# Gram operands of an RWKV-7 front made unswapped in one 128-partition product, swapped later by 64-column matmuls

## The chip, the cores and the metric

The kernel runs on one core of a Trainium2 chip. TensorE (PE) multiplies matrices; its weight loads are listed apart as PEld. VectorE (DVE) and ScalarE (ACT) work on tiles in on-chip memory, GpSimd (POOL) and SyncE (SP) mostly issue transfers. The metric is the time of one execution on the device, in microseconds (us); lower is better.

## The reference, cut to what matters

One decoder layer: an RWKV-7 branch and an S5 branch are merged by gates, and a gated MLP follows. The part around the change is the RWKV-7 recurrence, with 8 heads of 64 channels and 1024 time steps:

```python
def step(S, inp):
    r_t, w_t, k_t, v_t, a_t, b_t = inp
    sa = jnp.einsum('bhij,bhj->bhi', S, a_t)
    S = (S * w_t[:, :, None, :] + sa[..., None] * b_t[:, :, None, :]
         + v_t[..., None] * k_t[:, :, None, :])
    return S, jnp.einsum('bhij,bhj->bhi', S, r_t)
```

It is called with a = -kk and b = kk * a_gate, where kk is the key, scaled and normalised in each head, and with a key k that the gate has scaled as well. All numbers are float32.

## The kernel before, in words

The recurrence is computed in chunks of 64 time steps. In each chunk the products of all pairs of steps are needed: of the "b" and "k" vectors of step s with the "a" and "r" vectors of step t. These are the Gram matrices, 128 by 128 for a head and a chunk, since (b, k) and (a, r) are each laid side by side, 64 columns each.

The work is cut into four groups `d` (two halves of the sequence by two groups of four heads). A group holds two pairs of heads, `u` = 0 and 1, and eight chunks, `c` = 0 to 7. In a tile the first head of a pair (head 0) lies in partitions 0 to 63 and the second (head 1) in partitions 64 to 127; `HS[0]` and `HS[1]` are these two slices, of partitions or of columns.

`rwkv_front` (L680 ff.) runs once for each `d` and `u`, eight times in all. On DVE it writes `ar` (a in columns 0 to 63 of a chunk, r in 64 to 127: L736 and L726) and `bk` (b and k: L739 and L728). For head 0, b stands in columns 0 to 63 of `bk` and k in 64 to 127; for head 1 they stand the other way round. A DVE instruction writes the same columns in all its partitions, so L728 and L739 are each made of two instructions, one for each head, of 64 partitions by 512 elements.

Then PE makes the Gram matrices in two halves of four chunks (`q` = 0, 1): L750 issues, for each chunk, one product for head 0 and one for head 1, each with 64 rows of weights and 128 columns, 128 elements moving. DVE masks them into `gr` (L752), POOL sends parts of `gr` away (L758) for the inversion (`rwkv_inv`, on DVE).

`rwkv_nat` (L767 ff.) runs once for each `d`: for each `u` and `q`, PE transposes four chunks of `bk` (L780), ACT copies the result to `bkn` (L781), and PE does the same with v (L787, L788, L790), which ACT copies to `UV` (L792). Then `rwkv_level` and `rwkv_chain` run the recurrence over the chunks.

All matmul operands here are float32, and one such matmul makes two records in the trace; a transpose makes one. The large matmuls of the projections (L179 to L181) are of another type and make one record each.

The order of PE's instructions is written by `drive`: it hands the turn to several generators by their estimates of time (the numbers that they yield) and fills PE's free time with pieces of the projections. The instructions of one piece stay together. The order on the other engines comes from a scheduler.

Of the kernel before, what the change touches and what calls it, by code (L numbers as in the profile page):

```python
# [13 lines left out]
ALU = mybir.AluOpType  # L14
# [13 lines left out]
HS = (slice(0, 64), slice(64, 128))  # L28
# [44 lines left out]
class Kern:  # L73
# [606 lines left out]
    def rwkv_front(self, d, u, i):  # L680

        nc, V, G, A = self.nc, self.nc.vector, self.nc.gpsimd, self.nc.scalar
        mm = nc.tensor.matmul
        o = slice(d["th"] * 512, d["th"] * 512 + 512)
        p = 2 * d["g"] + u
        gf = d["gr"][:, u].rearrange("p c h t -> p (c h t)")
        kk, yb, pe = gf[:, 0:512], gf[:, 512:1024], gf[:, 1024:1544].rearrange("p (c t) -> p c t", t=65)

        def c64(x):
            return x.rearrange("p (c t) -> p c t", t=64)  # L690

        def ld(src, q=nc.sync):
            t = self.tg("ld", NLD)
            q.dma_start(t, src[:, o])
            return t
        k, tz, ta, r = (ld(x) for x in (self.RKV[4 + p], self.TZ[p], self.TA[p], self.RKV[p]))

        self.squared = A.activation(kk, k, AF.Square, scale=self.vec("k_k", p))
        if d["g"] == d["th"] == 0:
            self.tc.add_manual_dep(self.squared.ins, self.last_wh.ins.name, ORDER)  # L700
        yield 0, T_LD
        yield 0, lambda: self.nat >= i - 1 and self.outs >= i - 1
        if "ar" not in d:
            self.rwkv_operands(d)
        ar, bk = d["ar"][:, u], d["bk"][:, u]
        ar0, ar1 = ar[:, :, 0:64], ar[:, :, 64:128]
        bk0, bk1 = [[bk[HS[h], :, HS[h ^ j]] for h in range(2)] for j in range(2)]
        st = self.rp((128, 4, 2))
        for tb in range(4):
            mm(st[:, tb], kk[:, tb * 128:(tb + 1) * 128], self.cst("ones_bd")[:, 0:128:64], start=tb == 0, stop=True,  # L710
               skip_group_check=True)
        sv = self.small.tile([128, 8], F32, tag="sv", name=self.nm("sv"), bufs=2)
        V.tensor_scalar(sv, st.rearrange("p a b -> p (a b)"), 1e-24, None, ALU.max)
        y = self.rsqrt(sv, 8, "pr")

        scan = V.tensor_tensor_scan(tz, self.cst("smask"), tz, 0.0, ALU.mult, ALU.add)
        if self.levelled is not None:
            self.tc.add_manual_dep(scan.ins, self.levelled.ins.name, ORDER)
        G.memset(pe[:, :, 0:1], 1.0)
        A.activation(pe[:, :, 1:65], c64(tz), AF.Exp, scale=-0.5 * CDEC)  # L720
        A.activation(tz, tz, AF.Exp, scale=0.5 * CDEC)
        G.tensor_copy(d["pt"][:, :, u], pe[:, :, 64])
        tk = yb
        A.activation(tk, ta, AF.Identity, bias=self.ka_1[:, p:p + 1], scale=self.ka_h[:, p:p + 1])
        V.tensor_tensor(tk, tk, k, ALU.mult)
        V.tensor_tensor(ar1, c64(r), pe[:, :, 1:65], ALU.mult)  # L726
        for h, sl in enumerate(HS):
            V.tensor_tensor(bk1[h], c64(tk)[sl], c64(tz)[sl], ALU.mult)  # L728
        V.scalar_tensor_tensor(r, r, self.vec("r_k", p), tk, ALU.mult, ALU.mult)
        yield 0.9, T_KN, 1.5  # L730
        kb = self.rp()
        A.copy(c64(yb), y.unsqueeze(2).to_broadcast([128, 8, 64]))
        for tb in range(4):
            nc.tensor.transpose(kb[:, tb * 128:(tb + 1) * 128], yb[:, tb * 128:(tb + 1) * 128], self.cst("ident"))
        V.scalar_tensor_tensor(kk, k, self.vec("k_k", p), kb, ALU.mult, ALU.mult)
        V.scalar_tensor_tensor(ar0, c64(kk), -1.0, pe[:, :, 0:64], ALU.mult, ALU.mult)  # L736
        V.scalar_tensor_tensor(kk, ta, 1.0, kk, ALU.add, ALU.mult)
        for h, sl in enumerate(HS):
            V.scalar_tensor_tensor(bk0[h], c64(kk)[sl], 0.5, c64(tz)[sl], ALU.mult, ALU.mult)  # L739
        v = ld(self.RKV[8 + p], G)  # L740
        yield 0.5, T_BK

        gm = self.cst("gmask").unsqueeze(1).to_broadcast([128, 4, 128])
        for q in range(2):
            yield 0, lambda: self.now >= self.masked
            self.masked = self.now + 1.8 + T_GR
            ps = [self.rp((128, 4, 128)) for h in range(2)]
            for c in range(4 * q, 4 * q + 4):
                for h, sl in ((0, slice(0, 64)), (1, slice(64, 128))):
                    mm(ps[h][:, c % 4], bk[sl, c], ar[sl, c], start=c % 4 == 0, stop=True, skip_group_check=True)  # L750
            for h in range(2):
                V.tensor_tensor(d["gr"][:, u, 4 * q:4 * q + 4, h], ps[h], gm, ALU.mult)  # L752
            yield 1.8, T_GR
        for blk in range(2):
            md = d["md"][u, blk].rearrange("(c h) q t -> h q c t", h=2)
            for h in range(2):
                sl = slice(64 * h + 32 * blk, 64 * h + 32 * blk + 32)
                nc.gpsimd.dma_start(md[h], d["gr"][sl, u, :, h, 32 * blk:32 * blk + 32])  # L758

        pb = self.rp()  # L760
        mm(pb, self.cst("ones_bd"), r, start=True, stop=True)
        V.tensor_tensor(r, pb, v, ALU.mult)
        nc.gpsimd.dma_start(d["bv"][u], r)
        d["v"][u] = v
        yield 0.55, 1.5

    def rwkv_nat(self, d):  # L767

        nc, A = self.nc, self.nc.scalar
        mm = nc.tensor.matmul  # L770
        ident = self.cst("ident")
        o = slice(d["th"] * 512, d["th"] * 512 + 512)
        d["bkn"] = self.tg("bkn", 1, (128, 2, 8, 128))
        d["UV"] = self.tg("UV", 1, (128, 8, 2, 2, 64))
        for u in range(2):
            v = d["v"][u]
            for q in range(2):
                ps = self.rp((128, 4, 128))
                for c in range(4):
                    nc.tensor.transpose(ps[:, c], d["bk"][:, u, 4 * q + c], ident)  # L780
                A.copy(d["bkn"][:, u, 4 * q:4 * q + 4], ps)  # L781
                yield 0.5, 0
                ps = self.rp((128, 4, 128))
                for c in range(4):
                    b = 4 * q + c
                    if b == 0:
                        mm(ps[64:128, c], v[:, 0:64], ident, start=True, stop=True, skip_group_check=True)  # L787
                        mm(ps[0:64, c], v[:, 448:512], ident, start=True, stop=True, skip_group_check=True)  # L788
                    else:
                        nc.tensor.transpose(ps[:, c], v[:, 64 * b - 64:64 * b + 64], ident)  # L790
                for h in range(2):
                    A.copy(d["UV"][HS[1 - h], 4 * q:4 * q + 4, h, u], ps[HS[1 - h], :, HS[h]])  # L792
                yield 0.5, 0.8
# [1367 lines left out]
```

## Time and profile before

| what | value |
|---|---|
| time, median of 3 runs | 1545.53 us (1538.57 to 1547.73) |
| the profiled execution: its time, its span | 1553.39 us, 1551.6 us |
| busy: PE, DVE, ACT | 96%, 74%, 47% |
| fronts: first and last Gram record (L750) | 302.7 us, 609.2 us |
| `rwkv_nat`: first and last transpose of `bk` (L780) | 324.6 us, 681.0 us |
| mean granted clock of TensorE | 0.980 |

Times within the profile count from the span's start. A row of a group of instructions gives line, engine, operation, the tiles written and read, the shapes and the count; then, behind the bar, the busy time in us and the mean duration of one in ns; then the idle time before them and what ended it. For a matmul the shape of the weights comes first, rows by columns (64\*128), then the operand that moves. The durations of matmuls overlap, because they are pipelined, so what one costs is read from the distance of the starts in the timeline: there a row gives the start, the time to the end of the last record in it, and the count of records.

### The profile page before, as it was taken

What the parts mean: (1) busy time and instruction counts of PE and PEld (TensorE: products, weight loads), DVE (VectorE), ACT (ScalarE), POOL (GpSimd) and SP (SyncE); (2) the same over time, 40 slices, a digit from 0 to 9 for tenths busy, and PEclk for the clock granted to TensorE, in tenths of its full rate; (3) what the DMA queues carried; (4) which work ended last, traced back from release to release, by engine and by line L of the source; (5) the groups of instructions that cost most, each with busy time, mean ns of one, the idle gap of its engine ahead of it and who ended that gap; (6) DMA issues with size and microseconds to landing.
All of it is one profiled execution on the core that took longest, in us unless ns stands there. A gap on an engine that the chain in (4) does not pass through costs nothing.

```text
span 1551.6 us, 23464 instructions
## 1 busy us (share of the span) xinstructions
PE 1486.4 (96%) x8622; PEld 1186.8 (76%) x8622; DVE 1150.6 (74%) x2112; ACT 725.3 (47%) x1200; POOL 180.1 (12%) x340
## 2 busy tenths in 40 slices
PE   7997999999999998989999999999999999999997
PEld 5786888777677676666778788888888888788775
DVE  7878874756456486784668869788888887698667
ACT  6454543331353344546534456455555555443452
POOL 0022111123130214030110011000000000000000
PEclk9998999999999999999999999999999999999999
DMA  6354344343433446452355576233333336953722
GB/s 211 113 151 131 100 134 151 130 139 101 147 108 110 123 129 172 144 168 69 115 184 166 182 265 204 95 109 115 123 102 110 121 115 204 330 172 122 239 74 109
DMA packets 121124, 224.44 MB, mean 145 GB/s; under 512 B 30976, under 2 KB 37120, under 8 KB 121008
## 3 DMA queue, kind: packets, MB, share of 16 engines
q1 hardware_dynamic: 90144, 153.98, 31.9%
q0 software_dynamic: 21024, 64.71, 12.6%
q10 hardware_dynamic: 9840, 4.24, 1.0%
q8 instruction: 68, 1.11, 0.3%
q14 instruction: 48, 0.39, 0.1%
HBM read 163.37 MB, written 57.41 MB: 142 GB/s over the span
## 4 chain that ended last, share of the span: by engine, by line
PE 71%; DVE 12%; DMA 7%; issue 5%; ACT 4%; SPq 0%; POOL 0%; DVEq 0%; ACTq 0%; POOLq 0%
PE gm L179 9%; PE gm L180 8%; PE gm L181 7%; PE rp L1578 5%; PE rp L1580 5%; PE rp L1579 5%; DMA st<-in_w_down_dram 2%; PE mm L1578 2%; PE mm L1580 2%; PE mm L1579 2%; PE ch L180 2%; PE ch L179 2%; PE ch L181 2%; PE mm L179 2%; PE mm L180 2%
## 5 line engine op out<-in xcount | busy, mean ns | idle before, releaser
L179 PE MATMUL gm<-hh,wh 128*128 128x512 f32 x688 | 292.6, 425 | 2.7 <-DVE last L1046 2.0
L180 PE MATMUL gm<-hl,wh 128*128 128x512 f32 x688 | 273.6, 398 | 1.7 <-DVE hl L245 1.6
L181 PE MATMUL gm<-hh,wl 128*128 128x512 f32 x688 | 273.1, 397 | 0.0
L159 ACT CAST wh<-wf 128x512 fp32r<-128x512 f32 x178 | 109.8, 620 | 176.4 <-PE gm L180 99.7
L160 DVE TENSOR_TENSOR wl<-wf,wh 128x512 fp32r<-128x512 f32 x178 | 122.5, 692 | 87.6 <-ACT wh L159 86.2
L179 PEld LDWEIGHTS gm<-hh,wh 128*128 128x128 f32 x688 | 131.7, 191 | 36.1 <-ACT spt L893 2.4
L181 PEld LDWEIGHTS gm<-hh,wl 128*128 128x128 f32 x688 | 131.5, 191 | 29.2
L180 PEld LDWEIGHTS gm<-hl,wh 128*128 128x128 f32 x688 | 132.1, 192 | 25.9 <-DVE hl L245 3.5
L1756 PE MATMUL d<-xl,wh 128*128 128x512 f32 x308 | 120.4, 391 | 5.4 <-DVE xl L245 5.4
L1755 PE MATMUL d<-xh,wh 128*128 128x512 f32 x308 | 120.1, 390 | 0.0
L1757 PE MATMUL d<-xh,wl 128*128 128x512 f32 x308 | 119.9, 389 | 0.0
L1578 PE MATMUL rp<-t,h 128*128 128x512 f32 x252 | 98.3, 390 | 1.6 <-ACT p L1592 1.6
L1580 PE MATMUL rp<-t,l 128*128 128x512 f32 x252 | 98.1, 389 | 0.0
L1579 PE MATMUL rp<-t,h 128*128 128x512 f32 x252 | 98.0, 389 | 0.0
L1756 PEld LDWEIGHTS d<-xl,wh 128*128 128x128 f32 x308 | 57.8, 188 | 19.2 <-DVE xl L245 7.4
L245 DVE TENSOR_TENSOR l<-r,h 128x1024 fp32r<-128x1024 f32 (+1 forms) x40 | 38.9, 971 | 39.5 <-ACT h L244 39.4
L1755 PEld LDWEIGHTS d<-xh,wh 128*128 128x128 f32 x308 | 57.8, 188 | 12.3 <-DVE p L1707 0.2
L244 ACT CAST h<-r 128x1024 fp32r<-128x1024 f32 (+1 forms) x40 | 33.9, 849 | 70.7 <-PE rp L1579 67.0
L1757 PEld LDWEIGHTS d<-xh,wl 128*128 128x128 f32 x308 | 57.8, 188 | 11.9
L1599 DVE SCALAR_TENSOR_TENSOR y<-zv,vecs,y 128x1023 f32<-128x1023 f32 (+1 forms) x42 | 53.8, 1280 | 10.2 <-ACT y L1597 10.2
L1578 PEld LDWEIGHTS rp<-t,h 128*128 128x128 f32 x252 | 47.3, 188 | 12.2 <-ACT p L1592 2.5
L1580 PEld LDWEIGHTS rp<-t,l 128*128 128x128 f32 x252 | 47.3, 188 | 9.9
(473 smaller groups left out, 3338.0 us busy)
## 6 DMA issues: line engine op xcount, KB each, us to landing
r<-in_w_up_dram SPq DMA_DIRECT2D x42, 512.0 KB, 3.5
wf<-in_w_in_dram SPq DMA_DIRECT2D x72, 256.0 KB, 3.0
st<-in_w_down_dram SPq DMA_DIRECT2D x55, 256.0 KB, 4.5
st<-ACT SPq DMA_DIRECT2D x44, 256.0 KB, 4.2
ACT<-y POOLq DMA_DIRECT2D x21, 512.0 KB, 2.9
GT<-ev POOLq DMA_DIRECT2D x32, 256.0 KB, 3.4
wf<-in_w_br_dram SPq DMA_DIRECT2D x32, 256.0 KB, 2.7
wf<-in_w_out_dram SPq DMA_DIRECT2D x32, 256.0 KB, 2.8
```

The lines of the kernel that those rows point to most:

```text
L159: self.last_wh = nc.scalar.copy(h[:, :n], f[:, :n])
L160: low = nc.vector.tensor_tensor(l[:, :n], f[:, :n], h[:, :n].bitcast(F32), ALU.subtract)
L179: mm(ps, a, xh[k], start=a0, stop=False)
L180: mm(ps, a, xl[k], start=False, stop=False)
L181: mm(ps, b, xh[k], start=False, stop=z0)
L1578: mm(ps, wh[:, c], xh, start=first and k == 0, stop=False, skip_group_check=True)
L1579: mm(ps, wh[:, c], xl, start=False, stop=False, skip_group_check=True)
L1580: mm(ps, wl[:, c], xh, start=False, stop=k == 3, skip_group_check=True)
L1599: V.scalar_tensor_tensor(y[:, lag:], z[:, 0:1024 - lag], self.vec(nme, i), y[:, lag:], ALU.mult, ALU.add)
L1755: mm(ps, wh[:, c], xh[:, x], start=start, stop=False, skip_group_check=True)
L1756: mm(ps, wh[:, c], xl[:, x], start=False, stop=False, skip_group_check=True)
L1757: mm(ps, wl[:, c], xh[:, x], start=False, stop=stop, skip_group_check=True)
```

## The change

DVE writes `bk` unswapped, b in columns 0 to 63 and k in 64 to 127 for both heads, so that L728 and L739 become one instruction each, of 128 partitions by 512 elements. The swap of head 1 moves to PE.

In the Gram products head 0 keeps its one matmul of 64 by 128. Head 1 gets two of 64 by 64: the k columns give partitions 0 to 63 of the result, the b columns partitions 64 to 127.

In `rwkv_nat` each transpose of a chunk becomes three matmuls with a part of the identity matrix as the operand that moves: one for head 0 (64 rows by 128 columns of weights) and two for head 1 (64 by 64), which swap its halves.

```diff
-        bk0, bk1 = [[bk[HS[h], :, HS[h ^ j]] for h in range(2)] for j in range(2)]
+        bk0, bk1 = bk[:, :, 0:64], bk[:, :, 64:128]
...
-        for h, sl in enumerate(HS):
-            V.tensor_tensor(bk1[h], c64(tk)[sl], c64(tz)[sl], ALU.mult)
+        V.tensor_tensor(bk1, c64(tk), c64(tz), ALU.mult)
...
-        for h, sl in enumerate(HS):
-            V.scalar_tensor_tensor(bk0[h], c64(kk)[sl], 0.5, c64(tz)[sl], ALU.mult, ALU.mult)
+        V.scalar_tensor_tensor(bk0, c64(kk), 0.5, c64(tz), ALU.mult, ALU.mult)
...
-                for h, sl in ((0, slice(0, 64)), (1, slice(64, 128))):
-                    mm(ps[h][:, c % 4], bk[sl, c], ar[sl, c], start=c % 4 == 0, stop=True, skip_group_check=True)
+                kw = dict(start=c % 4 == 0, stop=True, skip_group_check=True)
+                mm(ps[0][:, c % 4], bk[HS[0], c], ar[HS[0], c], **kw)
+                for j in range(2):
+                    mm(ps[1][HS[j], c % 4], bk[HS[1], c, HS[1 - j]], ar[HS[1], c], **kw)
...
-                    nc.tensor.transpose(ps[:, c], d["bk"][:, u, 4 * q + c], ident)
+                    x = d["bk"][:, u, 4 * q + c]
+                    mm(ps[:, c, 0:64], x[HS[0]], ident[HS[0], HS[0]], start=c == 0, stop=True, skip_group_check=True)
+                    for j in range(2):
+                        mm(ps[HS[j], c, 64:128], x[HS[1], HS[1 - j]], ident[HS[1], HS[1]], start=False, stop=True, skip_group_check=True)
```

Three places in the order of instructions show it. In these rows the shape is that of the result, partitions by elements; "x2" stands for two alike in a row; `rp` is a bank of results, `gm` one of a projection.

PE at the first half of the first Gram of the program, before: the last projection matmuls ahead of it, and the first chunk (the last two rows come three more times).

```order
L181 MATMUL gm_2939<-hh_395,wl_2842 128x512
L179 MATMUL gm_2939<-hh_400,wh_2841 128x512
L180 MATMUL gm_2939<-hl_401,wh_2841 128x512
L181 MATMUL gm_2939<-hh_400,wl_2842 128x512
L750 MATMUL rp_2952<-ar_2733,bk_2734 128x128
L750 MATMUL rp_2953<-ar_2733,bk_2734 128x128
```

The same place now (again the last two rows come three more times; L748 is head 0, L750 head 1).

```order
L181 MATMUL gm_2935<-hh_395,wl_2840 128x512
L179 MATMUL gm_2935<-hh_400,wh_2839 128x512
L180 MATMUL gm_2935<-hl_401,wh_2839 128x512
L181 MATMUL gm_2935<-hh_400,wl_2840 128x512
L748 MATMUL rp_2948<-ar_2733,bk_2734 128x128
L750 MATMUL rp_2949<-ar_2733,bk_2734 64x128 x2
```

The place in the order is the same; head 1's one product of 64 by 128 has become two of 64 by 64, and products of the two sizes now alternate.

PE at the first piece of `rwkv_nat`, before: the transposes of four chunks of `bk`, then those of v.

```order
L181 MATMUL gm_3080<-hh_415,wl_3075 128x512
L780 MATMUL rp_3225<-csts,bk_2734 128x128 x4
L787 MATMUL rp_3231<-csts,ld_2883 64x128
L788 MATMUL rp_3231<-csts,ld_2883 64x128
L790 MATMUL rp_3231<-csts,ld_2883 128x128 x3
L179 MATMUL gm_3080<-hh_420,wh_3074 128x512
```

The same place now, from the fourth chunk on (the first two rows stand there three times before, behind the L181 of the projection).

```order
L781 MATMUL rp_3237<-csts,bk_2734 128x64
L783 MATMUL rp_3237<-csts,bk_2734 64x64 x2
L790 MATMUL rp_3251<-csts,ld_2880 64x128
L791 MATMUL rp_3251<-csts,ld_2880 64x128
L793 MATMUL rp_3251<-csts,ld_2880 128x128 x3
L179 MATMUL gm_3092<-hh_420,wh_3086 128x512
```

Four transposes have become twelve matmuls, in which the two sizes alternate; nothing else on PE changes its place, here or elsewhere.

DVE where the b columns of the first two fronts are written, before.

```order
L737 SCALAR_TENSOR_TENSOR gr_2606<-ld_2623,gr_2606 128x512
L739 SCALAR_TENSOR_TENSOR bk_2734<-gr_2606,ld_2612 64x8x64
L160 TENSOR_TENSOR wl_3069<-wf_3070,wh_3068 128x512
L739 SCALAR_TENSOR_TENSOR bk_2734<-gr_2606,ld_2621 64x8x64
L739 SCALAR_TENSOR_TENSOR bk_2734<-gr_2606,ld_2612 64x8x64
L739 SCALAR_TENSOR_TENSOR bk_2734<-gr_2606,ld_2621 64x8x64
L716 SCALAR_TENSOR_TENSOR ld_3032<-csts,ld_3032 128x512
```

The same place now.

```order
L736 SCALAR_TENSOR_TENSOR gr_2606<-ld_2623,gr_2606 128x512
L737 SCALAR_TENSOR_TENSOR bk_2734<-gr_2606,ld_2612 128x8x64
L160 TENSOR_TENSOR wl_3081<-wf_3082,wh_3080 128x512
L737 SCALAR_TENSOR_TENSOR bk_2734<-gr_2606,ld_2621 128x8x64
L716 SCALAR_TENSOR_TENSOR ld_3040<-csts,ld_3040 128x512
```

Two of four instructions are gone. Elsewhere some instructions of DVE and ACT, and a few transfers, change places with their neighbours.

## The prediction

> **What bounds the kernel now.** I read the page first: the busy times and the chain that ended last.
>
> ```profile
> PE 1486.4 (96%) x8622; PEld 1186.8 (76%) x8622; DVE 1150.6 (74%) x2112; ACT 725.3 (47%) x1200; POOL 180.1 (12%) x340
> PE 71%; DVE 12%; DMA 7%; issue 5%; ACT 4%; SPq 0%; POOL 0%; DVEq 0%; ACTq 0%; POOLq 0%
> ```
>
> PE is busy for 96% of the span and carries 71% of the chain. PE's order is fixed, and projection matmuls stand in every gap of the fronts, so a microsecond added to PE there ends up in the time, unless a wait of PE behind it shrinks. So the second view is PE's own waits between 290 and 800 us, where all fronts and all of `rwkv_nat` lie (in us: total, count, longest).
>
> ```profile
> PE rp L750 <- DVE bk L739: 5.9, 2, 5.5
> PE rp L959 <- DVE yn L951: 5.6, 1, 5.6
> PE rp L750 <- DVE ld L762: 2.7, 3, 1.8
> ...
> PE rp L734 <- ACT gr L732: 1.8, 1, 1.8
> PE rp L790 <- ACT UV L792: 1.3, 2, 0.7
> ```
>
> These are nearly all the waits around the change: 17.3 us together. They are the most that can be won back. The third view is the groups that the change touches.
>
> ```profile
> L750 PE MATMUL rp<-ar,bk 64*128 64x128 f32 x256 | 23.5, 304 | 9.0 <-DVE bk L739 5.9 <-DVE ld L762 2.7 <-DVE gr L752 0.3
> L739 DVE SCALAR_TENSOR_TENSOR bk<-gr,ld 64x512 f32<-64x512 f32 x16 | 10.8, 683 | 0.2
> L728 DVE TENSOR_TENSOR bk<-gr,ld 64x512 f32<-64x512 f32 x16 | 10.7, 683 | 0.3
> L780 PE MATMUL rp<-csts,bk 128*128 128x128 f32 x64 | 9.6, 272 | 0.0
> L736 DVE SCALAR_TENSOR_TENSOR ar<-gr 128x512 f32<-128x512 f32 x8 | 5.4, 685 | 0.1
> ```
>
> **DVE: what is removed.** An instruction over 128 partitions (L736, 685 ns) takes no longer than one over 64 (683 ns). So 32 instructions become 16, and DVE loses 16 x 0.685 = 11 us of work. DVE is not the bound; PE waits for `bk` only twice, 5.9 us in all. The pair of fronts ahead of the longer wait loses four instructions: 4 x 0.68 = 2.7 us. I take all of it: a gain of 2.7 us, with 0 and 5.9 as ends.
>
> **PE: the Gram products.** What counts is the distance of starts. The first half Gram, with the projection matmuls around it (start, time to the last end, records):
>
> ```profile
> 302.42 0.39 PE L181 MATMUL gm<-hh,wl 128*128 128x512 f32 x1
> 302.73 0.38 PE L750 MATMUL rp<-ar,bk 64*128 64x128 f32 x2
> ...
> 302.95 0.39 PE L750 MATMUL rp<-ar,bk 64*128 64x128 f32 x4
> ...
> 303.62 0.28 PE L750 MATMUL rp<-ar,bk 64*128 64x128 f32 x2
> 303.83 0.50 PE L179 MATMUL gm<-hh,wh 128*128 128x512 f32 x1
> ```
>
> The records come in pairs: the heads use different halves of the array's rows and run beside each other. The second pair starts 0.22 us after the first, the remaining six in 0.67 us (0.11 each), and the next projection 0.21 us after the last pair. So a half costs 303.83 - 302.73 = 1.10 us, and the edges, where the size of the products changes, are dear: 0.21 at the end and 0.11 of cold start.
>
> Is that so at every change of size? Around the two matmuls of 128 by 64 in `rwkv_nat`, and at a change from 64 by 64 to 64 by 128 (same number of rows):
>
> ```profile
> 324.60 0.60 PE L780 MATMUL rp<-csts,bk 128*128 128x128 f32 x4
> 325.12 0.32 PE L787 MATMUL rp<-csts,ld 128*64 128x128 f32 x1
> 325.13 0.32 PE L788 MATMUL rp<-csts,ld 128*64 128x128 f32 x1
> 325.28 0.27 PE L787 MATMUL rp<-csts,ld 128*64 128x128 f32 x1
> 325.29 0.27 PE L788 MATMUL rp<-csts,ld 128*64 128x128 f32 x1
> 325.49 0.33 PE L790 MATMUL rp<-csts,ld 128*128 128x128 f32 x1
> ...
> 502.50 0.23 PE L898 MATMUL chk<-S,ar 64*64 64x64 f32 x2
> 502.65 0.38 PE L750 MATMUL rp<-ar,bk 64*128 64x128 f32 x2
> ```
>
> Yes: 0.20 us from the last start of one size to the first of the next when 128 elements move (325.29 to 325.49), and 0.15 us when 64 move (502.50 to 502.65). Nothing of the new size starts while the old one runs.
>
> In the changed Gram each chunk has two such changes: a product of 64 by 128, then two of 64 by 64. The first stays 0.22 + 0.21 = 0.43 us, of which I take 0.42 (a single head lacks the pair's few ns). The two of 64 by 64 are nearest to L787 and L788, also a pair of 64 columns with 128 elements moving: 325.49 - 325.12 = 0.37 us. So a chunk takes 0.79 us, four take 3.15 us in place of 1.10, and there are 8 fronts x 2 halves: 16 x 2.05 = 33 us.
>
> That a product on rows 64 to 127 waits for one of another size on rows 0 to 63 no row shows: all changes of size here lie on rows that overlap. Ends: 0 us if it doesn't wait, 33 if it does. I take 33, by the row at 502.65, the nearest.
>
> The Trainium skill states both sides of it. "TensorEngine Tiling (Array Packing)", under "Tiling Modes", says that changing the tiling mode, not just the tile, drains TensorE; the rows above agree wherever the mode changes, and by it the sum is the one that I make. "TensorE: Matmul & The Clock Gate", under "Part 3: Packing small matmuls — row/col tiling", says that products on different groups of rows run at the same time, with starts about 4 ns apart; the pairs of L750 agree, and the third rival below is what it would give.
>
> **PE: the transposes.** Now, and the rows from which the new piece is built:
>
> ```profile
> 327.04 0.39 PE L181 MATMUL gm<-hh,wl 128*128 128x512 f32 x1
> 327.27 0.60 PE L780 MATMUL rp<-csts,bk 128*128 128x128 f32 x4
> 327.70 0.27 PE L790 MATMUL rp<-csts,ld 128*128 128x128 f32 x1
> ...
> 404.65 0.22 PE L867 MATMUL chk<-UV,gr 64*64 64x64 f32 x1
> 404.80 0.50 PE L179 MATMUL gm<-hh,wh 128*128 128x512 f32 x1
> ...
> 406.35 0.27 PE L896 MATMUL chb<-p,gr 64*64 64x64 f32 x2
> 406.38 0.27 PE L898 MATMUL chk<-S,ar 64*64 64x64 f32 x2
> 406.46 0.23 PE L896 MATMUL chb<-p,gr 64*64 64x64 f32 x2
> ```
>
> Four transposes cost 0.43 us. In their place each chunk has one product of 64 by 128 with 64 elements moving: 0.21 between its two records (the load of 128 columns sets that, as at 302.95) and 0.15 to the next size (404.65 to 404.80): 0.36 us. Then two of 64 by 64: 0.11 between records (406.35 to 406.46), 0.01 for the second, 0.15 to the next size: 0.27 us. Four chunks take 2.5 us. Coming from a projection costs 0.08 more (302.42 to 302.73 against 327.04 to 327.27), and the following L790 starts cold, 0.06 more (0.33 against 0.27). So 2.64 - 0.43 = 2.2 us for a piece, and 2.06 for the half of them that change size today already (324.60 to 325.12): 8 x 2.2 + 8 x 2.06 = 34 us.
>
> **What is given back.** Gross, PE gains 33 + 34 = 67 us of work. Against it stand the waits listed above. The one for `bk`: 2.7, as said. The ones for L762 (2.7) come behind a half Gram, and DVE has 2 us more to be done: 2.0. L792 (1.3) is ACT's copy inside `rwkv_nat`, which gets 2 us more as well: 1.3. The 5.6 us for L951 come behind the last `rwkv_nat`, whose four pieces will be 4 x 2.13 = 8.5 us longer; but DVE, which makes PE wait there, also evicts the projections that stand between the transposes and is held up with them: I take 1.0, with 0 and 5.6 as ends. Sum 7 us. DMA and the later stages come after and only shift.
>
> Net 67 - 7 = 60 us. The profiled execution took 1553.39 us (span 1551.6), 7.9 us above the median of 1545.53; against its own time the sum gives 1613, against the median 1605.
>
> **The rivals.**
>
> *The clock sags.* Where PE is sparsely used for some microseconds, it is granted half the clock (columns: stretch, length, PE busy and records, granted clock, DMA):
>
> ```profile
> 469.38:472.79 3.41, 3.41 (x62) 1.00 0.66 240
> 472.79:479.62 6.83, 6.83 (x35) 0.50 0.01 4
> ...
> 585.40:588.80 3.40, 0.35 (x2) 1.00 0.47 60
> 588.85:595.67 6.82, 4.38 (x20) 0.50 0.70 223
> ```
>
> The second time a wait of 5.5 us came before it; but the first time PE was filled with 62 small records. The new pieces are of that kind. Eight more such sags of 6.8 us, each costing up to 3.4, add 27: 1632 us. Against it: the halves last 2.5 to 3.2 us and dense projections stand between them.
>
> *Each record changes the size.* At 406.35 to 406.46 the two records of a float32 product are apart, with those of another product between them. If the records of both sizes are interleaved so, a chunk has four changes. With cold starts of 0.11 and, for 64 columns, 0.05 (325.12 to 325.28, less 0.11), a Gram chunk is then 2 x (0.11 + 0.20 + 0.05 + 0.01 + 0.20) = 1.14 us, a half 4.6, 3.5 more than now; a piece of transposes 2 x (0.11 + 0.15 + 0.05 + 0.01 + 0.15) x 4 = 3.8, 3.3 more. 16 x 6.8 = 109, less 7: 1647 us. Against it: there the products had one size; a queue that waits for the array to be empty would let the second record through first.
>
> *No waiting between halves of the rows* (the other side). If 64 by 64 on rows 64 to 127 runs beside 64 by 128 on rows 0 to 63, a half Gram stays at 1.10 us and costs nothing. A piece of transposes, at the same 0.11 us for each of eight records, takes a half Gram's 1.1 us: 1.1 + 0.14 - 0.43 = 0.8, and 16 x 0.8 = 13 us. Less 7: +6, so 1551 us, no change. It decides from the point where head 1 starts within 0.01 us of head 0 instead of 0.4 later. To get faster by 1%, all the 17 us of waits would have to go besides, and the 13 be hidden.
>
> *The change doesn't do what it says*, for instance because the weights of the next size are loaded while the last product runs: then the cold starts (0.11 and 0.05 for each of 128 chunks, 20 us) are saved, 1585 us. That lies in the forecast's own range.
>
> **How the numbers follow.** Forecast (waits at each change of size) 0.66; clock 0.10; four changes 0.07; no waiting 0.14; faster for a reason that I don't see 0.03. The forecast's own range is 1580 to 1625. With the clock and the four changes it reaches to 1650 and holds 0.66 + 0.10 + 0.07 = 0.83, less a little at the low end: about 0.8. Left out are the 0.17 of the two cases below. A measurement of this kernel tells 1% from no change. Faster by over 1%: 0.03; within 1%: 0.14; slower by over 1%: 0.83.
>
> **What would show it.** Right: in the timeline of a half Gram, records of 64\*128 and 64\*64 alternate, with starts about 0.4 us apart and 3.15 us in all; a piece of transposes takes 2.6 us; L739's successor has 8 instructions of 685 ns; PE's waits for `bk` shrink to about 3 us. Wrong: head 1's records start with head 0's, or the four chunks take near 1.1 us; a clock at half for many more stretches; PE waits behind `rwkv_nat` that vanish by more than 7 us.

## The result, and the profile after

The changed kernel takes 1621.38 us (median of 6 runs, 1616.76 to 1632.24); the kernel before took 1547.99 us in its six runs beside it (1538.57 to 1551.42). The ratio is 1.050, with a 95% interval of 1.047 to 1.053: slower by 73 us. 1605 was forecast, with 1580 to 1650 as the range.

The profiled execution has a span of 1630.4 us, 79 us more than that of before. On the page of the changed kernel, the busy times and the row of granted clocks (40 slices, in tenths):

```profile
PE 1577.7 (97%) x9070; PEld 1241.6 (76%) x9070; DVE 1143.0 (70%) x2096; ACT 727.4 (45%) x1200; POOL 180.7 (11%) x340
PEclk9998999989998999797999999999999999999999
```

PE is busy for 91 us more and DVE for 8 us less. The first half Gram in the timeline of the changed kernel (start, time to the last end, records); L748 is head 0, L750 head 1:

```profile
301.31 0.39 PE L181 MATMUL gm<-hh,wl 128*128 128x512 f32 x1
301.63 0.48 PE L748 MATMUL rp<-ar,bk 64*128 64x128 f32 x2
302.04 0.44 PE L750 MATMUL rp<-ar,bk 64*64 64x128 f32 x4
302.41 0.37 PE L748 MATMUL rp<-ar,bk 64*128 64x128 f32 x1
...
304.75 0.50 PE L179 MATMUL gm<-hh,wh 128*128 128x512 f32 x1
```

Head 1 starts 0.41 us behind head 0, and the next chunk 0.37 us behind head 1: 0.78 us for a chunk, 304.75 - 301.63 = 3.12 us for a half, where it had been 1.10. The rows of the two heads do not overlap, and still the second size waits until the first is through. A piece of transposes:

```profile
331.87 0.43 PE L781 MATMUL rp<-csts,bk 64*128 64x64 f32 x2
332.23 0.33 PE L783 MATMUL rp<-csts,bk 64*64 64x64 f32 x4
332.49 0.32 PE L781 MATMUL rp<-csts,bk 64*128 64x64 f32 x1
...
334.10 0.33 PE L783 MATMUL rp<-csts,bk 64*64 64x64 f32 x4
334.36 0.32 PE L790 MATMUL rp<-csts,ld 128*64 128x128 f32 x1
```

Here 0.36 and 0.26 us, 2.49 us for the piece. And DVE writes each of the two column halves of `bk` with one instruction for each front. The b columns (count; shortest, median, longest in ns; first and last start):

```profile
L737 DVE SCALAR_TENSOR_TENSOR bk<-gr,ld x8: 682/686/691, 296.3 to 638.1; 128x512 f32<-128x512 f32 x8
```

The waits of PE between 290 and 860 us (total, count, longest):

```profile
PE rp L750 <- DVE ld L762: 6.7, 4, 5.5
PE chk L888 <- ACT p L874: 2.4, 4, 0.9
PE chk L888 <- DVE S L913: 2.1, 2, 1.2
PE chk L901 <- ACT p L874: 1.5, 1, 1.5
```

The wait for `bk` is gone, and so is the one for `yn` (L951 before); one of 5.5 us stands in front of a Gram product still, but it is for another DVE result, L762. All eight rows of this answer sum to 15.2 us; the fifteen of before, for 290 to 800 us, to 28.3. So 13 us were given back. They did not all come from where they were expected: the waits in front of the Gram products, for `bk` and for L762, were 5.9 and 2.7 and are 0 and 6.7, so that 1.9 us of their 8.6 are won.

The rest goes with the clock. The stretch from 260 to 860 us in both kernels (length, PE busy and records, granted clock, DMA), before and after:

```profile
260.00:860.00 600.00, 569.64 (x4381) 0.97 0.46 139
```

```profile
260.00:860.00 600.00, 582.12 (x4470) 0.91 0.37 114
```

The clock is granted in full or by half (no other value stands in these traces), so a mean of 0.97 is about 0.03 x 2 x 600 = 36 us at half clock, and 0.91 is about 108 us: 72 us more, of which half speed can lose half. Both profiles lie at the low end of their kernel's runs: over the whole span they have 0.980 and 0.962. The six runs of the changed kernel lie between 0.962 and 0.971, and all runs of the kernel before for which a clock is on record between 0.980 and 0.992, so the difference is not of these two executions alone. Two places where it happened in the changed kernel, and the start of a piece of transposes in the first of them:

```profile
343.20:347.60 4.40, 4.40 (x27) 0.50 0.00 0
658.90:682.80 23.90, 19.99 (x111) 0.50 0.19 57
```

```profile
343.50 0.69 PE L781 MATMUL rp<-csts,bk 64*128 64x64 f32 x2
344.12 0.48 PE L783 MATMUL rp<-csts,bk 64*64 64x64 f32 x4
344.52 0.47 PE L781 MATMUL rp<-csts,bk 64*128 64x64 f32 x1
```

At half clock a chunk of the transposes takes 344.52 - 343.50 = 1.02 us in place of 0.62, and the projections around it go at half speed too. Five of the sixteen pieces ran so from end to end. The second place is less plain: its half clock begins inside the 5.5 us wait for L762 (PE stands still from 657.3 to 662.8 us), and the Gram products follow it.

So the 79 us of the two profiled executions are: 16 x 2.03 = 32 for the Gram halves, 8 x 2.06 + 8 x 1.96 = 32 for the transposes, some 2 for entering and leaving them, less 13 for waits that shrank, and by difference some 26 for the clock. That this difference is the clock's alone is not shown; it lies under the 36 us that the half clock can cost.

### The profile page after: what moved, and what is told of

The parts are those of the page before. It is cut to its first block, busy times and chain, and to the rows that moved or that the text cites. A ratio compares the mean times of both kernels' runs of the same rounds, so it can differ in the third digit from the quotient of the medians.

```text
span 1630.4 us, 24334 instructions
## 1 busy us (share of the span) xinstructions
PE 1577.7 (97%) x9070; PEld 1241.6 (76%) x9070; DVE 1143.0 (70%) x2096; ACT 727.4 (45%) x1200; POOL 180.7 (11%) x340
## 3 DMA queue, kind: packets, MB, share of 16 engines
q0 software_dynamic: 21024, 64.71, 11.8%
## 4 chain that ended last, share of the span: by engine, by line
PE 40%; DVE 5%; DMA 3%; issue 2%; ACT 1%; SPq 0%; DVEq 0%; ACTq 0%
PE rp L1581 5%; PE rp L1583 5%; PE rp L1582 5%; DMA st<-in_w_down_dram 2%; PE mm L1581 2%; PE mm L1582 2%; PE mm L1583 2%; PE ch L180 2%; PE ch L181 2%; PE ch L179 2%; PE mm L179 2%; PE mm L180 2%; PE mm L181 2%; PE d L1759 1%; PE d L1760 1%
## 5 line engine op out<-in xcount | busy, mean ns | idle before, releaser
L179 PE MATMUL gm<-hh,wh 128*128 128x512 f32 x688 | 299.2, 435 | 3.4 <-DVE last L1049 2.6
L180 PE MATMUL gm<-hl,wh 128*128 128x512 f32 x688 | 280.2, 407 | 1.7 <-DVE hl L245 1.6
L181 PE MATMUL gm<-hh,wl 128*128 128x512 f32 x688 | 279.5, 406 | 0.0
L181 PEld LDWEIGHTS gm<-hh,wl 128*128 128x128 f32 x688 | 135.6, 197 | 30.6
L180 PEld LDWEIGHTS gm<-hl,wh 128*128 128x128 f32 x688 | 135.5, 197 | 26.5 <-DVE hl L245 3.7
```

The costliest lines, as they stand in the source:

```text
L179: mm(ps, a, xh[k], start=a0, stop=False)
L180: mm(ps, a, xl[k], start=False, stop=False)
L181: mm(ps, b, xh[k], start=False, stop=z0)
```

## The experiments

Two theories stood against each other. **A**: each change between sizes of product empties the array and starts it cold, and the cost goes with the number of changes. **B**: the cost goes with the number of matmuls and records. Each ratio below is to runs of the kernel before on the same chip, with its 95% interval.

**One size, Gram and transposes.** The DVE part of the change stays. Head 0's Gram product is split as well, so that all Gram products are 64 by 64; the transposes are those of 128 by 128 again, and their swap goes to ACT.

```diff
-                mm(ps[0][:, c % 4], bk[HS[0], c], ar[HS[0], c], **kw)
+                for j in range(2):
+                    mm(ps[0][HS[j], c % 4], bk[HS[0], c, HS[j]], ar[HS[0], c], **kw)
...
+                    nc.tensor.transpose(ps[:, c], d["bk"][:, u, 4 * q + c], ident)
+                A.copy(d["bkn"][:, u, 4 * q:4 * q + 4, 0:64], ps[:, :, 0:64])
+                for j in range(2):
+                    A.copy(d["bkn"][HS[j], u, 4 * q:4 * q + 4, 64:128], ps[HS[1 - j], :, 64:128])
```

> The unswapped bk stays (DVE has 16 instructions fewer). Gram: head 0 is also made as two products of 64 by 64, so that all products of a half have one size; transposes: four of 128 by 128 again, and the swap is made by ACT, in three copies in place of one. Theory A (each change of size empties the array, about 0.2 us and a cold start): a half Gram falls from 3.12 us to about 1.1 although it has 32 records in place of 24, a piece of transposes from 2.49 to 0.44, and the time is within 5 us of the kernel before, at best 3 us below it (DVE's relief). Theory B (the cost goes with the number of matmuls and records): a half Gram takes 3.12 x 32/24 = 4.2 us, and the time stays near 1600 us.

Measured: 1547.18 us against 1546.85, ratio 1.0004 (0.9987 to 1.0021). The whole loss is gone, although a half Gram has 32 records in place of 24. But the transposes have fewer here (the whole kernel 8878 records against 9070), so theories A and B are told apart by the Gram alone, in the next run.

**One size, Gram alone.** The first hunk of the diff above, the transposes as changed.

> The changed kernel, but head 0's Gram product is also made as two of 64 by 64; the transposes stay as changed. Theory A: a half Gram at 1.1 us, 16 x 2.0 = 32 us less than the changed kernel, and a little more by fewer stretches at half clock: 1580 to 1590 us. Theory B: 4.2 us for a half, 16 x 1.0 more than the changed kernel: 1635 us.

Measured: 1587.36 us, ratio 1.027 (1.024 to 1.031). The timeline of its first half Gram (L749 head 0, L751 head 1):

```profile
296.97 0.39 PE L181 MATMUL gm<-hh,wl 128*128 128x512 f32 x1
297.29 0.33 PE L749 MATMUL rp<-ar,bk 64*64 64x128 f32 x2
297.30 0.33 PE L751 MATMUL rp<-ar,bk 64*64 64x128 f32 x2
297.44 0.28 PE L749 MATMUL rp<-ar,bk 64*64 64x128 f32 x2
297.46 0.28 PE L751 MATMUL rp<-ar,bk 64*64 64x128 f32 x2
...
298.11 0.28 PE L751 MATMUL rp<-ar,bk 64*64 64x128 f32 x2
298.32 0.50 PE L179 MATMUL gm<-hh,wh 128*128 128x512 f32 x1
```

All four quadrants of the array start within 0.01 to 0.02 us of each other and go on every 0.11 us. The half takes 298.32 - 297.29 = 1.03 us with 32 records, where 24 records of two sizes took 3.12. Theory B, with 4.2 us and 1635, falls.

**Each part of PE's change alone, on the kernel before.** First head 1's Gram product split, without a swap:

```diff
-                for h, sl in ((0, slice(0, 64)), (1, slice(64, 128))):
-                    mm(ps[h][:, c % 4], bk[sl, c], ar[sl, c], start=c % 4 == 0, stop=True, skip_group_check=True)
...
+                mm(ps[0][:, c % 4], bk[HS[0], c], ar[HS[0], c], **kw)
+                for j in range(2):
+                    mm(ps[1][HS[j], c % 4], bk[HS[1], c, HS[j]], ar[HS[1], c], **kw)
```

> The kernel before, with its swapped bk and its transposes; only head 1's Gram product is made as two of 64 by 64 (no swap is needed). Theory A: 16 x 2.03 = 32 us over before, 1575 to 1590 us. If the clock's sags belong to the Gram halves, more of them, up to 1600. If the two changes were only slow together: under 1560.

Measured: 1585.44 us, ratio 1.028 (1.024 to 1.032).

Then only the transposes by parts of the identity:

```diff
-                    nc.tensor.transpose(ps[:, c], d["bk"][:, u, 4 * q + c], ident)
...
+                    mm(ps[:, c, 0:64], x[HS[0]], ident[HS[0], HS[0]], start=c == 0, stop=True, skip_group_check=True)
+                    for j in range(2):
+                        mm(ps[HS[j], c, 64:128], x[HS[1], HS[j]], ident[HS[1], HS[1]], start=False, stop=True, skip_group_check=True)
```

> The kernel before with only the transposes of bk made of three matmuls with parts of the identity (without the swap). Theory A: 8 x 2.05 + 8 x 1.96 = 32 us over before, 1575 to 1585 us, and since five of the sixteen changed pieces ran wholly at half clock in the changed kernel, some 10 to 15 us more by sags: 1585 to 1595. Without sags of its own: 1580.

Measured: 1587.44 us, ratio 1.029 (1.025 to 1.033). The parts cost 39 and 41 us; together 79, where the whole change costs 73. They add up, within what DVE's relief and the intervals leave open. Each part costs 7 to 9 us more than its 32 us of pieces; the rest was not taken apart for the single parts.

**The transposes undone, Gram as changed** (the second hunk of the first diff).

> The changed kernel with the transposes of 128 by 128 again and the swap made by ACT in three copies; Gram as changed. Theory A: 16 x 2.0 = 32 us less than the changed kernel, and 5 to 10 more by sags that go with the transposes: 1578 to 1590 us, near the kernel before with only its Gram split (1585).

Measured: 1579.97 us, ratio 1.021 (1.016 to 1.026), 41 us less than the changed kernel. On PE it does the same work as the kernel before with only its Gram split, which took 1585.44. The 5 us between them are no finding: the intervals of the two ratios overlap, and the like pair for the transposes (Gram in one size, 1587.36, and the kernel before with parts of the identity, 1587.44) shows no difference.

**The same products, grouped by size.** In each half Gram and each piece of transposes all of head 0's products come first; there is one change inside where there were seven.

```diff
...
+            for c in range(4 * q, 4 * q + 4):
+                mm(ps[0][:, c % 4], bk[HS[0], c], ar[HS[0], c], **kws[c % 4])
+            for c in range(4 * q, 4 * q + 4):
+                for j in range(2):
+                    mm(ps[1][HS[j], c % 4], bk[HS[1], c, HS[1 - j]], ar[HS[1], c], **kws[c % 4])
...
```

> The changed kernel with the same products, but in each half Gram and each piece of transposes head 0's four come first and head 1's eight behind them: the changes of size inside fall from seven to one. Theory A (price per change): a half Gram takes 0.21 + 6 x 0.11 + 0.20 for head 0 and 0.16 + 6 x 0.11 + 0.21 for head 1, 2.1 us in place of 3.12; a piece of transposes 1.0 + 0.6 = 1.6 us in place of 2.49. 16 x (1.0 + 0.9) = 30 us less than the changed kernel, and some sags less: 1580 to 1592 us. If instead each product has its own price, whatever its neighbours are: unchanged, 1621.

Measured: 1560.50 us, ratio 1.010 (1.006 to 1.015). The timeline of its first half Gram and its first piece of transposes:

```profile
299.67 1.16 PE L748 MATMUL rp<-ar,bk 64*128 64x128 f32 x8
300.75 1.09 PE L751 MATMUL rp<-ar,bk 64*64 64x128 f32 x16
301.77 0.50 PE L179 MATMUL gm<-hh,wh 128*128 128x512 f32 x1
...
324.16 1.10 PE L782 MATMUL rp<-csts,bk 64*128 64x64 f32 x8
325.19 0.68 PE L785 MATMUL rp<-csts,bk 64*64 64x64 f32 x16
325.80 0.32 PE L792 MATMUL rp<-csts,ld 128*64 128x128 f32 x1
```

The half takes 301.77 - 299.67 = 2.10 us and the piece 325.80 - 324.16 = 1.64, as theory A had it. (Transposes made of products of one size were not run, so for them the price per change rests on this piece.) But the time missed the expectation on the low side: it fell by 61 us, twice the 30 that the pieces account for. The clock goes with the rest, in the same stretch as above:

```profile
260.00:860.00 600.00, 586.62 (x4799) 0.99 0.44 136
```

About 12 us at half clock in place of 108, of which half speed can lose half, 48. Its four runs lie between 0.984 and 0.991 over the whole span, the six of the changed kernel between 0.962 and 0.971. So the price of the changes comes twice: once as empty time on PE, and again as clock.

**More projections between the transposes.**

```diff
                 A.copy(d["bkn"][:, u, 4 * q:4 * q + 4], ps)
-                yield 0.5, 0
+                yield 0.5, 2.5
```

> The changed kernel, but the generator of rwkv_nat waits 2.5 us of its estimated time behind each piece of transposes of bk, so that some 12 more projection matmuls stand there; all products stay as they are. If the stretches at half clock come from sparse pieces that follow each other too closely, fewer of the sixteen pieces run at half clock (five did) and 5 to 12 us are won: 1609 to 1616 us. If the sags do not depend on it: 1621, or slower because the chain starts later.

Measured: 1623.97 us, ratio 1.052 (1.047 to 1.056): no gain over the changed kernel. In its profile all sixteen pieces ran at full clock, 2.49 us each, and the stretch had a mean clock of

```profile
260.00:860.00 600.00, 578.00 (x4522) 0.95 0.38 117
```

that is about 60 us at half clock in place of 108. But this profile is of the fastest of the four runs, with 0.977 over the whole span; the others had 0.967 to 0.974, hardly more than the changed kernel, whose own profile is of its slowest run. So in this profile the pieces were helped; over the runs the clock hardly was, and the time not at all. The chain starts later, and what that costs was not separated.

**DVE's part alone.** The kernel before with `bk` written as in the changed kernel; head 1's swap is left out, so that this kernel computes something else and serves for its time alone.

```diff
-        for h, sl in enumerate(HS):
-            V.tensor_tensor(bk1[h], c64(tk)[sl], c64(tz)[sl], ALU.mult)
+        V.tensor_tensor(bk1, c64(tk), c64(tz), ALU.mult)
...
```

> The kernel before with bk written unswapped by 16 instructions fewer; the swap of head 1 is left out altogether, so that PE's work is word for word that of the kernel before. Theory: the wait for bk shrinks by 2.7 us and nothing else changes: 1542 to 1547 us, 0 to 0.3% faster. If PE's wait there is passed on to the next wait in line: no difference.

Measured: 1541.86 us against 1546.33, ratio 0.998 (0.996 to 1.000): about 3.4 us by the ratio, at the edge of what twelve runs can tell. The first two rows of PE's waits in it (L748 is the Gram there, L750 its masking):

```profile
PE rp L957 <- DVE yn L949: 5.6, 1, 5.6
PE rp L748 <- DVE gr L750: 3.3, 2, 2.9
```

No row for `bk` is left; a part of its 5.9 us has become a wait of 3.3 for the masking of the Gram.

Why did the first experiment not keep these 3.4 us? Its waits suggest a reason:

```profile
PE rp L793 <- ACT UV L795: 2.4, 2, 1.9
...
PE rp L781 <- ACT UV L795: 1.6, 1, 1.6
PE rp L781 <- ACT bkn L784: 1.2, 1, 1.2
```

5.2 us for ACT's copies in `rwkv_nat`, where the kernel before had 1.3 and 0.4: three copies in a piece have replaced one. That is not the whole account: all waits between 290 and 800 us sum to 24.5 us here and to 22.2 with DVE's part alone, 2.3 more. To test it, one of the three copies went to DVE:

```diff
-                for j in range(2):
-                    A.copy(d["bkn"][HS[j], u, 4 * q:4 * q + 4, 64:128], ps[HS[1 - j], :, 64:128])
+                A.copy(d["bkn"][HS[0], u, 4 * q:4 * q + 4, 64:128], ps[HS[1], :, 64:128])
+                nc.vector.tensor_copy(d["bkn"][HS[1], u, 4 * q:4 * q + 4, 64:128], ps[HS[0], :, 64:128])
```

> As the run with both parts undone on PE (unswapped bk, Gram in one size, transposes of 128 by 128), but of the three copies that make the swap one goes to DVE, which has 11 us less to do, so that ACT's path behind a piece of transposes is shorter by 0.37 us. DVE alone gave 3.4 us; if ACT's copies took that back, this gives 1 to 3 us: 1543 to 1546. If it was lost elsewhere: no difference from the kernel before.

Measured: 1549.36 us against 1546.02, ratio 1.002 (1.000 to 1.004). No gain: a miss. The waits for the copies of `rwkv_nat` only fell from 5.5 us in all to 4.1, and a wait of 4.6 us for the masking of a Gram product appeared. So where DVE's relief is lost stays open. No version of this swap that was tried beats the kernel before.

**Fewer changes of size elsewhere.** Does the price per change make time where the kernel before has changes of its own? In `rwkv_level` four pieces of 32 by 32 products, with projections between them, become one.

```diff
-                    if c % 4 == 3:
-                        yield 0.3, 0.3, 2.0
                 for h in range(2):
                     evict(u, h)
-            yield 0, T_LV
+            yield 1.2, T_LV, 2.0
```

> The kernel before, with its bk and its Gram; only in rwkv_level the products of 32 by 32 of one step (64 records) stand together instead of in four pieces of 16 with projection matmuls between them, which takes three of four changes of size away. Theory A: a piece of 16 costs 0.37 us and 0.09 on entry, four cost 1.84; 64 records together at 0.017 each and one exit about 1.2. 8 steps x 0.65 = 5 us less than the kernel before: 1541 us. If the projection matmuls between the pieces hide something that now waits (ACT's copies, DVE): no gain, or a loss of a few us.

Measured: 1547.04 us against 1546.02, ratio 1.001 (0.999 to 1.003). No gain. Three of the four pieces of L836 did become shorter (1.13 us for 64 records, where four pieces of 16 took 4 x 0.37 = 1.48), but those of L838, the other four of the eight steps, became longer (2.15 us and more, with a wait inside). Four rows of its waits:

```profile
PE chk L838 <- ACT gr L839: 5.4, 4, 2.1
PE chk L901 <- DVE UV L897: 4.5, 3, 2.9
PE gm L179 <- ACT hh L249: 3.7, 1, 3.7
PE chk L883 <- ACT p L869: 3.1, 3, 1.4
```

Before, the first was 2.1, the second 0.9, the third not there, the fourth 1.9: 11.8 us more in these four. Others shrank, the one for `bk` to nothing, so that all waits between 290 and 800 us grew by 4.3 us, from 28.3 to 32.6: about the 5 us that were to be won. The first row shows the mechanism, here in one of its four places: the second half of L838's products waits for ACT's copy (L839) of the first half's result.

```profile
388.63 0.69 PE L838 MATMUL chk<-gr,ld 32*32 32x32 f32 x32
390.16 0.69 PE L838 MATMUL chk<-gr,ld 32*32 32x32 f32 x32 [0.83 <-ACT gr L839]
```

In the kernel before, projection matmuls stand between the pieces and hide most of this copy.

## Why the prediction was right, and where it was short

*What bounds the kernel*: right. PE's added work appears in the time, except for what waits gave back.

*DVE*: right in kind; the size is not settled. 2.7 us were taken, 3.4 measured for DVE's part alone (interval 0.2 to 6.8), and the unswapped `bk` with PE's work in one size showed no gain.

*The Gram products*: right. 0.79 us for a chunk was forecast, 0.78 measured; 3.15 for a half, 3.12 measured. The step that no row before could show, that rows 64 to 127 wait for another size on rows 0 to 63, is now shown at 301.63 and 302.04, and by the two opposites: 1.03 us with one size, 2.10 with one change.

*The transposes*: 2.5 us forecast for the matmuls, 2.49 measured, but two errors cancel. The product of 64 by 128 has its second record 0.16 us behind the first, not 0.21, and leaves 0.20 to the next size, not 0.15: with 64 elements moving, the exit of 128 columns of weights is as long as with 128 elements moving. That the sum came out is luck here.

*What is given back*: 7 us forecast, 13 found in the waits, and from other places. The wait for `yn` was taken to shrink by 1.0 and went altogether (5.6). The two in front of the Gram products were to give 4.7 and gave 1.9: the one for `bk` went, but the one for L762, of which 2.0 us were to go, grew by 4.0.

*The rivals*. No waiting between halves of the rows: refuted in the changed kernel's own timeline. (Products of one size do run side by side there; their starts lie 7 ns apart in a pair, not the 4 that the prediction quotes.) Four changes in a chunk: refuted too; the rows show both records of a size (x2, x4) before the next. That the change doesn't do what it says: no; no weights are loaded ahead of a change, each starts cold. The weight loads of the two sizes (PEld) begin at 302.04 and 302.41, when their first products do:

```profile
302.04 0.20 PEld L750 LDWEIGHTS rp<-ar,bk 64*64 64x64 f32 x4
302.41 0.18 PEld L748 LDWEIGHTS rp<-ar,bk 64*128 64x128 f32 x1 [0.17 <-issue]
```

*The clock*: this is the term that was mis-sized. It was put aside as a rival with a chance of 0.10, at 27 us, on the ground that "the halves last 2.5 to 3.2 us and dense projections stand between them". That did not hold: some 26 us went this way in the profiled execution, by difference, and the median lies 16 us above the forecast; without the 6 us that the waits gave back beyond the forecast it would lie higher. Part of the rival came true beside the forecast, not in its place. The two should have been added from the start: pieces whose matmuls stand 0.15 to 0.20 us apart at every change, 32 of them, are near to the kind that the rows at 469 us had shown.

## What to carry to other kernels

Price a matmul by its neighbours: a product of another size next to it costs 0.15 to 0.20 us of emptying and a cold start, even on rows of the array that the other leaves free, and 64 by 64 products beside 64 by 128 ones cost more than splitting all of them to 64 by 64. Group products by size, and count the changes before and after an edit, as one counts instructions; but where other work between pieces hides copies, merging the pieces gains nothing. Where PE is the bound, 11 us less on DVE gave about 3 us, and with two more copies a piece in its place no gain was left.

## What the runs showed of the hardware that was not expected

The granted clock fell while PE counted as busy. PE counted as busy for 95% and 97% of the stretches compared here (570 and 582 of 600 us), yet the mean clock went from 0.97 to 0.91 when products of two sizes alternated, and to 0.99 when the same products were grouped. That it answers to the empty time at the changes is the nearest reading, but it is not shown: grouping makes the pieces shorter as well, and one of the half-clock stretches begins in a wait. What share of emptiness, over what time, brings the clock down was not measured, and spreading the pieces did not make the kernel faster.

Four quadrants of one size are a little faster than two halves: 1.03 us for a half Gram of 32 records of 64 by 64, against 1.10 for 16 records of 64 by 128. The cold start is shorter with 64 columns of weights: 0.15 us to the second record (297.29 to 297.44), against 0.22.
